# One more column pair by eleven block products in a two-layer streaming encoder step, and a reordered feed of its last projection

## The chip, the core and the metric

The kernel runs on one core of a Trainium2 chip. The metric is device time in microseconds (us) from launch to end, the median of three runs. Beside it stands one profiled execution, with its own time and its span from the first to the last instruction. TensorE is written PE in the rows, its weight load PEld, VectorE DVE, ScalarE ACT, GpSimd POOL, SyncE SP.

## The reference, cut to what matters

Two layers act on 384 token rows: 256 of a prompt (two blocks of 128) and 128 of running streams (one block). Layer 0 is attention of two kinds. Layer 1 is the one that the change touches:

```python
def c_project(h, w_in1, ln_g, ln_b):
    p = jnp.einsum('bsd,dn->bsn', h, w_in1)          # 2048 x 12288
    u = p[..., :C_WIDTH]                             # C_WIDTH = 4096
    v = layernorm(p[..., C_WIDTH:2 * C_WIDTH], ln_g, ln_b)
    z = p[..., 2 * C_WIDTH:]
    return u, v, z
...
mixed = spatial_mix(v, w_sp, b_sp)                   # 128 x 128 causal mixing, 16 groups
hp = hp + jnp.einsum('bsn,nd->bsd', u * mixed * jax.nn.silu(z), w_out1)   # 4096 x 2048
```

So layer 1 is one wide projection, a small mixing of positions, and a second projection back to 2048 columns, added to the layer's input (the residual).

## The kernel before, in words

**Precision.** All inputs are 32-bit floats. Each operand is split in a high and a low half in the matmul's own 32-bit format: ScalarE copies the high half, VectorE subtracts to get the low half, and TensorE adds three products (high by high, high by low, low by high). For 128-row weight blocks of 512 columns that is `wunit` (L79 to L86: `whi` by ScalarE on L84, `wlo` by VectorE on L86) and `products` (L100 to L102). Three token blocks by three products make 9 matmuls for one weight block.

**Column pairs by eleven products.** In layer 1 the weight is taken two column blocks of 512 at a time (columns a0 and a1). For the two prompt blocks, seven products do the work of eight, in the manner of Strassen and Winograd; the stream block needs four ordinary ones, so a pair takes eleven block products where two ordinary column blocks take twelve. This is `seven` (from L959). A product is one token block by half of the 16 weight blocks, 8 of them, by three matmuls: 24 matmuls. Each pair has three parts, each of four units u:

- *singles*: products 1, p, 2 and q; per unit two loads of 128 x 1024, two splits, 24 matmuls;
- *chain*: products 5, s (first half), 6 and 4; per unit four loads, three adds of 128 x 1024 on VectorE (`add`, L968) and three splits, 24 matmuls;
- *pair*: products 3, s (second half) and 7; per unit two loads, one add, two splits, 18 matmuls.

The splits are made by `split` through `split2`: the high half `shi` on L90 (ScalarE), the low half `slo` on L91 (VectorE). Four buffers hold each; the loads (`sraw`) have eight. The parts end with adds that read the product banks. The first of those after the chain reads product 6, and the adds of the pair part are put behind it (`issue_after(second[0])`).

Three pairs are of v columns (`v_pair`), and NP = 5 pairs each join a z block with a u block (`zu_pair`). What is left of z and u is done in ordinary 128-row units (`eight`): four column blocks, z5, u5, z6 and u6, 64 units, loaded through GpSimd's queue. They are dealt out among the units of the chain and the pair parts by the table `mix`, and a scheduler with its own estimates then fixes the order of each engine; no engine reorders at run time. In the built program some 30 ordinary matmuls stand between the chain and the pair part of each pair, where product 6 is awaited, and the rest is spread over the chain and over the start of the next pair.

**The last part.** z7 and u7 are two ordinary column blocks (L1279 to L1285). Meanwhile the gate groups c = 0 to 7 are prepared by generators, `prepare(c)`, eight steps each: loads, three of normalising v, turned mixing weights (L1194), split values, mixing matmuls and gate (L1229 to L1233), stores of the gated rows to DRAM and their read back in blocks (L1236 and L1239, GpSimd's queue), then a turn on VectorE (`gTt`, L1243) and its split into the left operand of the second projection (`slot`, L90 and L91). Tables of hook numbers (`first_plan`, `later_plan`) say behind which weight block a step is written. `out1(k0, nk)` (L1173) runs the second projection over weight rows of two gate groups at a time, four column blocks each, and adds the result to h1 (L1178); h1 comes back from DRAM by `residual_back` on SyncE's queue.

Of the kernel before, what the change touches and what calls it, by code (L numbers as in the profile page):

```python
# [15 lines left out]
P = 128  # L16
DM = 2048
KT = DM // P
NT = 3
# [18 lines left out]
def tile_hybrid_step(  # L38
# [8 lines left out]
    V, S, G, PE = nc.vector, nc.scalar, nc.gpsimd, nc.tensor  # L47
# [121 lines left out]
    with ExitStack() as l0:  # L169
# [200 lines left out]
        for strict in (0, 1):  # L370
# [4 lines left out]
            md = lc.tile([P, TW], F32, name=f"md{strict}")  # L375
# [491 lines left out]
    with ExitStack() as l1:  # L867
# [9 lines left out]
        with ExitStack() as lv:  # L877
# [205 lines left out]
            evict_v(1, dense_nat(w_in1, 0, CW + 512, hh_, hl_, KT, between={kp: lambda q=q: token_sums(q) for q, kp in enumerate((2, 6, 10, 14))}))  # L1083
            NP = 5
            ordinary = [st for c in range(NP, 7) for st in eight(evict_z, c, 2 * CW + c * 512) + eight(evict_u, c, c * 512)]

# [75 lines left out]
        ghi, glo, fgs, aside = [], [], [], {}  # L1162
# [6 lines left out]

        def gk(x, k):  # L1170
            return x[k // 4][:, k % 4, :]

        def out1(k0, nk, between=None):  # L1173
            for c in range(4):
                o = dense_nat(w_out1, k0, c * 512, [gk(ghi, k) for k in range(k0, k0 + nk)], [gk(glo, k) for k in range(k0, k0 + nk)],
                              between={kp: lambda: between.pop(0)() for kp in range(0, nk, 2)} if between else None)
# [32 lines left out]
        def prepare(c):  # L1209
# [24 lines left out]
            yield  # L1234
            for tb in range(NT):
                G.dma_start(md[c][:, tb * P:(tb + 1) * P, :].rearrange("k t d -> t k d"), gate[:, tb, :].rearrange("p (k d) -> p k d", k=4))  # L1236
            blk = lp.tile([P, 4, T], F32, tag="trn", name=nm("blk"))
            for j in range(4):
                G.dma_start(blk[32 * j:32 * j + 32].rearrange("p k (a d) -> p (k a) d", d=32),  # L1239
                            md[c][:, :, 32 * j:32 * j + 32].rearrange("k (a p) d -> p (k a) d", p=32))  # L1240
            yield
# [5 lines left out]
            glo.append(lo)  # L1247

        preps = [prepare(c) for c in range(8)]

# [11 lines left out]
        def times(c, *whens):  # L1262
            return [(c, i) for i in whens]
# [22 lines left out]
        for k0 in (0, 8, 16):  # L1286
            if k0 == 16:
                for j in range(2):
                    fg = slot(F32)[:, :1024]
                    G.dma_start(fg, final_g[j * 1024:(j + 1) * 1024].partition_broadcast(P))  # L1290
                    fgs.append(fg)

                x = slot(F32).rearrange("p (j c) -> p j c", j=3)
                for j, ck in enumerate(order[:3]):
                    aside[ck] = x[:, j, :]
                    G.dma_start(x[:, j, :], wlast(*ck))
            out1(k0, 8, hooked(later_plan(k0 // 4 + 2)))
        wl = {}
# [11 lines left out]

        evicted = out1(24, 4, [lambda: None] * 2 + [last_split] * 3 + [lambda: None] * 3)

# [18 lines left out]
        def last(tb, i):  # L1331
# [4 lines left out]
            for k in range(KL):  # L1336
                hi, lo = wl[c, k]
                gh, gl = gk(ghi, 32 - KL + k)[:, t], gk(glo, 32 - KL + k)[:, t]
# [71 lines left out]
```

## Time and profile before

| | |
|---|---|
| median of three runs | 1756.29 us (1756.17 to 1760.43) |
| profiled execution, its own time | 1759.73 us |
| its span, first to last instruction | 1758.0 us |
| TensorE busy | 1737.2 us, 99% |
| VectorE busy | 1225.6 us, 70% |
| ScalarE, GpSimd busy | 792.6 us, 395.9 us |
| mean granted clock | 0.996 |
| read from memory, written | 357.70 MB, 48.29 MB |

Matmuls are pipelined: a matmul of 512 columns is shown with 390 ns, though the next starts earlier, so the starts give the pace. Idle time stands behind an instruction in brackets with what ended it. The pairs of layer 1 run from about 780 us to 1400 us, z7 and u7 to about 1462 us, the second projection from there to the end.

### The profile page before, as it was taken

The page shows a single profiled execution, that of the slowest core. Times are in us where ns is not written, and L with a number is a line of the kernel's source. Part 1 is how long each engine was busy: PE and PEld are TensorE (multiplying, and loading weights), DVE is VectorE, ACT ScalarE, POOL GpSimd, SP SyncE. Part 2 cuts the span into 40 slices and gives each one's busy share as a digit, 9 for nine tenths or more (in the row PEclk, how much of TensorE's full clock was granted, in tenths as well). Part 3 has the DMA queues.
Part 4 walks back from the last instruction along what each step waited for, and adds up shares of the span by engine and source line. Part 5 has one row for each costly group of instructions (what it writes and reads, how often), then busy time and mean ns, then how long its engine had stood idle before and what let it go on. Part 6 is the DMA issues. An engine that isn't in the chain of part 4 may idle for free. (4 is left out here: it accounts for less than half of the span.)

```text
span 1758.0 us, 24054 instructions
## 1 busy us (share of the span) xinstructions
PE 1737.2 (99%) x8371; PEld 1438.3 (82%) x8371; DVE 1225.6 (70%) x1752; ACT 792.6 (45%) x1239; POOL 395.9 (23%) x581
## 2 busy tenths in 40 slices
PE   9999999999999999999999999999999998999998
PEld 8978888888888888888888888888888887887877
DVE  6437565448348455588788888888788877787766
ACT  5435354337336344454454444545445343333334
POOL 6425545222212201110210010000000233332200
PEclk9999999999999999999999999999999999999999
DMA  8788989868877876678788788877878788878653
GB/s 231 189 222 186 273 228 220 242 178 207 239 200 194 262 197 154 182 272 283 245 262 293 235 281 280 259 262 243 273 258 276 260 271 255 247 223 249 181 144 116
DMA packets 223210, 407.63 MB, mean 232 GB/s; under 512 B 22552, under 2 KB 66128, under 8 KB 223088
## 3 DMA queue, kind: packets, MB, share of 16 engines
q1 hardware_dynamic: 157584, 278.84, 52.7%
q0 software_dynamic: 34672, 111.12, 22.6%
q10 hardware_dynamic: 30832, 16.13, 3.1%
q8 instruction: 65, 1.06, 0.3%
q14 instruction: 57, 0.47, 0.1%
HBM read 357.70 MB, written 48.29 MB: 231 GB/s over the span
## 5 line engine op out<-in xcount | busy, mean ns | idle before, releaser
L101 PE MATMUL d<-wlo,slot 128*128 128x512 f32 x1581 | 616.6, 390 | 2.2 <-DVE wlo L86 2.2
L102 PE MATMUL d<-whi,slot 128*128 128x512 f32 x1581 | 615.2, 390 | 0.0
L100 PE MATMUL d<-whi,slot 128*128 128x512 f32 x1581 | 568.7, 392 | 9.1 <-ACT slot L90 6.1
L86 DVE TENSOR_TENSOR wlo<-raw,whi 128x512 fp32r<-128x512 f32 x514 | 351.7, 696 | 313.3 <-ACT whi L84 309.2
L84 ACT ACTIVATE whi<-raw 128x512 fp32r<-128x512 f32 x514 | 321.6, 629 | 522.1 <-PE d L102 439.0
L100 PEld LDWEIGHTS d<-whi,slot 128*128 128x128 f32 x1581 | 296.8, 188 | 76.1 <-ACT slot L90 6.5
L101 PEld LDWEIGHTS d<-wlo,slot 128*128 128x128 f32 x1581 | 297.4, 188 | 65.2 <-DVE wlo L86 4.3
L102 PEld LDWEIGHTS d<-whi,slot 128*128 128x128 f32 x1581 | 297.0, 188 | 62.0 <-DVE slot L278 0.3
L90 ACT ACTIVATE shi<-sraw 128x1024 fp32r<-128x1024 f32 x224 | 234.7, 1059 | 231.5 <-PE a L957 182.0
L91 DVE TENSOR_TENSOR slo<-sraw,shi 128x1024 fp32r<-128x1024 f32 x224 | 269.2, 1220 | 47.5 <-ACT shi L90 45.2
L956 PE MATMUL a<-slo,slot 128*128 128x512 f32 x640 | 249.0, 389 | 0.0
L955 PE MATMUL a<-shi,slot 128*128 128x512 f32 x640 | 239.7, 389 | 0.0
L957 PE MATMUL a<-shi,slot 128*128 128x512 f32 x544 | 211.6, 389 | 0.0
L968 DVE TENSOR_TENSOR sraw<-sraw,sraw 128x1024 f32<-128x1024 f32 x128 | 154.1, 1220 | 28.3 <-DMA sraw<-in_w_in_dram 28.0
L956 PEld LDWEIGHTS a<-slo,slot 128*128 128x128 f32 x640 | 120.1, 188 | 25.0
L955 PEld LDWEIGHTS a<-shi,slot 128*128 128x128 f32 x640 | 120.1, 188 | 25.0
L74 POOL DMA_DIRECT2D raw<-in_w_in_dram x64 | 35.0, 546 | 397.4 <-DVE wlo L86 375.7
L957 PEld LDWEIGHTS a<-shi,slot 128*128 128x128 f32 x544 | 102.1, 188 | 21.2
L464 POOL DMA_DIRECT2D slot<-d x48 | 44.0, 924 | 140.2 <-DVE wlo L86 54.0
L563 POOL DMA_DIRECT2D slot<-wd x32 | 27.1, 855 | 89.4 <-DMA wd<-pr 41.4
L968 DVE TENSOR_TENSOR slot<-a,slot 128x512 f32<-128x512 f32 x56 | 37.6, 684 | 13.5 <-PE a L957 13.5
L1178 DVE TENSOR_TENSOR slot<-d,slot 128x512 f32<-128x512 f32 x48 | 32.0, 686 | 11.0 <-PE d L102 10.9
(315 smaller groups left out, 1671.3 us busy)
## 6 DMA issues: line engine op xcount, KB each, us to landing
sraw<-in_w_in_dram SPq DMA_DIRECT2D x256, 512.0 KB, 4.9
raw<-in_w_in_dram SPq DMA_DIRECT2D x320, 256.0 KB, 4.0
raw<-in_w_out_dram SPq DMA_DIRECT2D x175, 256.0 KB, 4.2
raw<-in_w_in_dram POOLq DMA_DIRECT2D x64, 256.0 KB, 5.4
slot<-d POOLq DMA_DIRECT2D x48, 192.0 KB, 5.7
d<-slot ACTq DMA_DIRECT2D x24, 256.0 KB, 3.7
vd<-slot POOLq DMA_DIRECT2D x8, 768.0 KB, 6.7
gd<-slot POOLq DMA_DIRECT2D x8, 768.0 KB, 7.3
```

What stands on the lines that cost most here:

```text
L84: highs.append(S.activation(hi, raw, AF.Copy).ins)
L86: splits.append(V.tensor_tensor(out=lo, in0=raw, in1=f32(hi), op=ALU.subtract).ins)
L90: S.activation(hi_out, src, AF.Copy)
L91: V.tensor_tensor(out=lo_out, in0=src, in1=f32(hi_out), op=ALU.subtract)
L100: PE.matmul(o, lhsT=his[k][:, t], rhs=hi[:, 0, :], start=(k == first), stop=False)
L101: PE.matmul(o, lhsT=his[k][:, t], rhs=lo[:, 0, :], start=False, stop=False)
L102: mm = PE.matmul(o, lhsT=los[k][:, t], rhs=hi[:, 0, :], start=False, stop=(k == last))
L464: r = G.dma_start(blk[32 * j:32 * j + 32].rearrange("p h (a d) -> p (h a) d", d=32), d[:, :, 32 * j:32 * j + 32].rearrange("h (a p) d -> p ...
L955: PE.matmul(o, lhsT=xh, rhs=hi[:, j, :], start=(opens and u + j == 0), stop=False)
L956: PE.matmul(o, lhsT=xh, rhs=lo[:, j, :], start=False, stop=False)
L957: PE.matmul(o, lhsT=xl, rhs=hi[:, j, :], start=False, stop=(ends and u == 3 and j == 1))
L968: return V.tensor_tensor(out=out, in0=x, in1=y, op=op)
```

## The change

NP becomes 6: a ninth pair (z5 with u5), and only z6 and u6, 32 units, remain ordinary. `mix` deals one unit to each chain unit (in every third pair three of four) and none to the pair part. In the last part the hook tables are moved: the turn of an odd group goes from the last hook of one `out1` to the second hook of the next (`Late` looks the operand up only when it is used), group 7's turn to the second hook of `out1(24, 4)`; the stores of a group's gated rows are put behind the read back of the group before (`issue_after` on `read`); and the residual comes back later.

```diff
-            NP = 5
+            NP = 6
...
-            for make, c in [(v_pair, c) for c in (2, 4, 6)] + [(zu_pair, c) for c in range(NP)]:
+            for n, (make, c) in enumerate([(v_pair, c) for c in (2, 4, 6)] + [(zu_pair, c) for c in range(NP)]):
...
-                for i, mix in ((1, (2, 2, 2, 1)), (2, (1, 0, 0, 0))):
+                for i, mix in ((1, (1, 1, 1, n % 3 != 1)), (2, (0, 0, 0, 0))):
...
-            for tb in range(NT):
-                G.dma_start(md[c][:, tb * P:(tb + 1) * P, :].rearrange("k t d -> t k d"), gate[:, tb, :].rearrange("p (k d) -> p k d", k=4))
+            with ExitStack() as behind:
+                for i in read:
+                    behind.enter_context(tc.issue_after(i))
+                for tb in range(NT):
+                    G.dma_start(md[c][:, tb * P:(tb + 1) * P, :].rearrange("k t d -> t k d"), gate[:, tb, :].rearrange("p (k d) -> p k d", k=4))
...
-        first_plan = [times(0, 0, 4, 5, 6, 7, 8, 9, 12), times(1, 2, 7, 8, 9, 10, 11, 12, 15), times(2, 13)]
+        first_plan = [times(0, 0, 4, 5, 6, 7, 8, 9, 13), times(1, 2, 7, 8, 9, 10, 11, 12), times(2, 12, 14, 15)]
...
-            return [times(c, 0, 1, 2, 3, 5, 6, 10), times(c + 1, 1, 4, 7, 8, 9, 11, 12, 15)] + ([times(c + 2, 13)] if c < 6 else [])
+            return [times(c - 1, 1), times(c, 2, 3, 5, 6, 13), times(c + 1, 2, 6, 7, 9, 10, 11, 12)] + ([times(c + 2, 10, 14, 15)] if c < 6 else [])
...
-        for i, c in ((5, 0), (7, 1), (9, 2), (11, 3)):
+        for i, c in ((10, 0), (13, 1)):
...
+            for i, c in ((2, 2), (6, 3)) if k0 == 0 else ():
...
-        evicted = out1(24, 4, [lambda: None] * 2 + [last_split] * 3 + [lambda: None] * 3)
+        evicted = out1(24, 4, [lambda: None, lambda: next(preps[7], None)] + [last_split] * 3 + [lambda: None] * 3)
```

The built programs show where the ordinary units went. Counting pairs from 0, the sixteen units of z6 stand before the second unit of pair 1's pair part, fifteen units of u6 between the start of pair 4 and the first units of pair 5's pair part, and the last one from the end of pair 8's chain on. From there in pair 1 to the start of pair 4, and from there in pair 5 to the end of pair 8's chain, TensorE's order has no ordinary matmul: 597 and 774 matmuls of pairs in a row (a pair has 264).

**First place: from the chain to the pair part.** In the program before, TensorE's order in pair 6; `slo_11788` is the low half of the pair part's first weight, `wlo` and `whi` belong to ordinary units:

```order
L956 MATMUL a_11496<-slo_11788,slot_6596 128x512
L957 MATMUL a_11496<-shi_11787,slot_6597 128x512
L955 MATMUL a_11496<-shi_11787,slot_6596 128x512
L956 MATMUL a_11496<-slo_11788,slot_6596 128x512
L957 MATMUL a_11496<-shi_11787,slot_6597 128x512
L101 MATMUL d_11472<-wlo_12084,slot_6999 128x512
L102 MATMUL d_11472<-whi_12082,slot_7000 128x512
L100 MATMUL d_11473<-whi_12082,slot_6999 128x512
L101 MATMUL d_11473<-wlo_12084,slot_6999 128x512
L102 MATMUL d_11473<-whi_12082,slot_7000 128x512
```

The same place in the changed program, again pair 6; `slo_11337` is the low half of the first added weight (product 7), `slo_11333` that of the weight before it:

```order
L956 MATMUL a_11077<-slo_11333,slot_6596 128x512
L957 MATMUL a_11077<-shi_11332,slot_6597 128x512
L955 MATMUL a_11077<-shi_11332,slot_6596 128x512
L956 MATMUL a_11077<-slo_11333,slot_6596 128x512
L957 MATMUL a_11077<-shi_11332,slot_6597 128x512
L955 MATMUL a_11326<-shi_11336,slot_7400 128x512
L955 MATMUL d_11325<-shi_11345,slot_7471 128x512
L955 MATMUL a_11077<-shi_11345,slot_6830 128x512
L956 MATMUL a_11326<-slo_11337,slot_7400 128x512
```

Three matmuls that need high halves alone now stand where the ordinary ones stood; then comes the first that needs the low half. From the last matmul of product 6 to that one there are 21 steps in pairs 3, 6 and 7, and 19 in pair 2.

VectorE's order at this place in the changed program; `a_11078` is product 6:

```order
L968 TENSOR_TENSOR slot_10915<-a_11078,slot_10915 128x512
L968 TENSOR_TENSOR sraw_11329<-sraw_11327,sraw_11329 128x1024
L968 TENSOR_TENSOR sraw_11342<-sraw_11340,sraw_11342 128x1024
L968 TENSOR_TENSOR sraw_11373<-sraw_11371,sraw_11373 128x1024
L968 TENSOR_TENSOR slot_10915<-a_11076,slot_10915 128x512
L968 TENSOR_TENSOR slot_10914<-slot_10915,a_11079 128x512
L968 TENSOR_TENSOR sraw_11404<-sraw_11402,sraw_11404 128x1024
L91 TENSOR_TENSOR slo_11337<-sraw_11329,shi_11336 128x1024
```

Before, the same eight instructions stood here, with the four wide adds next to each other; nothing else moved.

**Second place: GpSimd's queue in the last part.** Before, with `md_7087` the gated rows of group 0, `md_7088` those of group 1, and `blk` the read back:

```order
L1236 DMA md_7087<-gate_12581 128x4x128 x3
L1129 DMA v_13273<-vd_7074 128x1536
L1236 DMA md_7088<-gate_12655 128x4x128 x3
L1239 DMA blk_12941<-md_7087 32x48x32 x4
L1215 DMA gate_13127<-gd_7081 128x1536
L1239 DMA blk_13087<-md_7088 32x48x32 x4
```

And in the changed program:

```order
L1245 DMA md_7087<-gate_12573 128x4x128 x3
L1129 DMA v_13301<-vd_7074 128x1536
L1248 DMA blk_12921<-md_7087 32x48x32 x4
L1245 DMA md_7088<-gate_12647 128x4x128 x3
L1221 DMA gate_13071<-gd_7081 128x1536
L1248 DMA blk_13061<-md_7088 32x48x32 x4
```

The read of group 0 moved ahead of the stores of group 1.

**Third place: VectorE at the start of the second projection.** Before, from the last eviction of u7 (L1284) to the turn of group 1 (the L1243 that ends the piece):

```order
L1284 SCALAR_TENSOR_TENSOR slot_12572<-d_12881,rstd,slot_12572 128x512
L86 TENSOR_TENSOR wlo_13291<-raw_13287,whi_13289 128x512
L86 TENSOR_TENSOR wlo_13297<-raw_13293,whi_13295 128x512
L1140 SCALAR_TENSOR_TENSOR v_13122<-v_13122,mvr,lg_13124 128x512
L1194 STREAM_TRANSPOSE wT_13320<-wr_13129 128x512
L91 TENSOR_TENSOR slot_13081<-gTt_13078,slot_13080 128x1536
L1141 SCALAR_TENSOR_TENSOR v_13122<-v_13122,rsv,lg_13124 128x512
L1195 TENSOR_TENSOR wT_13320<-wT_13320,tri 128x256
L1243 STREAM_TRANSPOSE gTt_13196<-blk_13087 128x1536
```

In the changed program the eviction is L1294 and the turn L1252; the piece between them is longer, and its second half is

```order
L1141 SCALAR_TENSOR_TENSOR v_13066<-v_13066,rsv,lg_13068 128x512
L1201 TENSOR_TENSOR wT_13294<-wT_13294,tri 128x256
L86 TENSOR_TENSOR wlo_13319<-raw_13315,whi_13317 128x512
L86 TENSOR_TENSOR wlo_13325<-raw_13321,whi_13323 128x512
L91 TENSOR_TENSOR vl_13346<-v_13066,vh_13345 128x512 x3
L91 TENSOR_TENSOR wTl_13298<-wT_13294,wTh_13297 128x512
L86 TENSOR_TENSOR wlo_13357<-raw_13353,whi_13355 128x512
L1252 STREAM_TRANSPOSE gTt_13251<-blk_13061 128x1536
```

Group 0's turn moved ahead of the three evictions of u7; ahead of group 1's turn there now stand three more `wlo`, the three `vl`, one `wTl` and two small products of mixing weights (L1194).

More of the change, by code (lines that the diff above doesn't have):

```diff
@@ L1167, in wlast, with __init__, __getitem__ @@
             return w_out1[(32 - KL + k) * P:(33 - KL + k) * P, c * 512:(c + 1) * 512]
-        def gk(x, k):
-            return x[k // 4][:, k % 4, :]
+        class Late:
+            def __init__(self, x, k0):
+                self.x, self.k0 = x, k0
+            def __getitem__(self, k):
+                k += self.k0
+                return self.x[k // 4][:, k % 4, :]
         def out1(k0, nk, between=None):
             for c in range(4):
-                o = dense_nat(w_out1, k0, c * 512, [gk(ghi, k) for k in range(k0, k0 + nk)], [gk(glo, k) for k in range(k0, k0 + nk)],
+                o = dense_nat(w_out1, k0, c * 512, Late(ghi, k0), Late(glo, k0), nk,
                               between={kp: lambda: between.pop(0)() for kp in range(0, nk, 2)} if between else None)
@@ L1234, in prepare @@
             yield
-            for tb in range(NT):
-                G.dma_start(md[c][:, tb * P:(tb + 1) * P, :].rearrange("k t d -> t k d"), gate[:, tb, :].rearrange("p (k d) -> p k d", k=4))
+            with ExitStack() as behind:
[3 more added lines that the diff above has]
+                    G.dma_start(md[c][:, tb * P:(tb + 1) * P, :].rearrange("k t d -> t k d"), gate[:, tb, :].rearrange("p (k d) -> p k d", k=4))
             blk = lp.tile([P, 4, T], F32, tag="trn", name=nm("blk"))
             for j in range(4):
-                G.dma_start(blk[32 * j:32 * j + 32].rearrange("p k (a d) -> p (k a) d", d=32),
-                            md[c][:, :, 32 * j:32 * j + 32].rearrange("k (a p) d -> p (k a) d", p=32))
+                read[:] = [G.dma_start(blk[32 * j:32 * j + 32].rearrange("p k (a d) -> p (k a) d", d=32),
+                                       md[c][:, :, 32 * j:32 * j + 32].rearrange("k (a p) d -> p (k a) d", p=32)).ins]
             yield
@@ L1247, in prepare @@
             glo.append(lo)
+        read = []
         preps = [prepare(c) for c in range(8)]
@@ L1296, in tile_hybrid_step @@
                     G.dma_start(x[:, j, :], wlast(*ck))
-            out1(k0, 8, hooked(later_plan(k0 // 4 + 2)))
+            h = hooked(later_plan(k0 // 4 + 2))
+            for i, c in ((2, 2), (6, 3)) if k0 == 0 else ():
+                h[i] = lambda f=h[i], c=c: [residual_back(c), f()] and None
+            out1(k0, 8, h)
         wl = {}
@@ L1337, in last @@
                 hi, lo = wl[c, k]
-                gh, gl = gk(ghi, 32 - KL + k)[:, t], gk(glo, 32 - KL + k)[:, t]
+                gh, gl = Late(ghi, 32 - KL)[k][:, t], Late(glo, 32 - KL)[k][:, t]
                 PE.matmul(o, lhsT=gh, rhs=hi[:, cs], start=(k == 0), stop=False)
```

## The prediction

> **What bounds the kernel now.** I read the page first, then what TensorE waits for, then the stage of the pairs (TensorE's and VectorE's rows around one part of a pair), then the last part.
>
> The page's head, and from the list of TensorE's waits the two longest (us in total, times, longest):
>
> ```profile
> span 1758.0 us, 24054 instructions
> PE 1737.2 (99%) x8371; PEld 1438.3 (82%) x8371; DVE 1225.6 (70%) x1752; ACT 792.6 (45%) x1239; POOL 395.9 (23%) x581
> ```
>
> ```profile
> PE d L100 <- ACT slot L90: 6.1, 1, 6.1
> PE d L101 <- DVE wlo L86: 2.2, 4, 1.2
> ```
>
> TensorE is the bound and hardly stands still: its longest wait is one of 6.1 us, in the last part. A matmul that goes away is worth its pace, as long as the others keep coming. So two things decide: how many matmuls go, and whether the new order opens holes. The stage of the pairs, one stretch of 100 us (busy PE, PEld, DVE, ACT, POOL, clock, DMA share, GB/s), and from its groups the two wide ones on VectorE:
>
> ```profile
> 1000.00:1100.00 100.00, 100.00 (x443) 82.80 (x442) 86.25 (x94) 47.78 (x54) 11.09 (x20) 1.00 0.83 273
> ```
>
> ```profile
> L91 DVE TENSOR_TENSOR slo<-sraw,shi 128x1024 fp32r<-128x1024 f32 x224 | 269.2, 1220 | 47.5 <-ACT shi L90 45.2
> L968 DVE TENSOR_TENSOR sraw<-sraw,sraw 128x1024 f32<-128x1024 f32 x128 | 154.1, 1220 | 28.3 <-DMA sraw<-in_w_in_dram 28.0
> ```
>
> No hole in TensorE there, but VectorE is at 86%: 224 splits and 128 adds for 8 pairs, 44 wide instructions a pair. It is the engine to watch when a block that costs it little is turned into a pair.
>
> **The work that goes.** z5 and u5 as ordinary blocks are 2 x 144 = 288 matmuls, as a pair 11 x 24 = 264: 24 fewer. The pace, from TensorE's rows at the end of a chain (product 6's last matmul, the last of the weight after it, the first ordinary one, the first with an added weight's low half):
>
> ```profile
> 1298.78 0.39 PE L957 MATMUL a<-shi,slot 128*128 128x512 f32 x1
> ...
> 1302.86 0.39 PE L957 MATMUL a<-shi,slot 128*128 128x512 f32 x1
> 1303.09 0.39 PE L101 MATMUL d<-wlo,slot 128*128 128x512 f32 x1
> ...
> 1311.48 0.39 PE L956 MATMUL a<-slo,slot 128*128 128x512 f32 x1
> ```
>
> From 1298.78 to 1302.86 are 18 steps, 0.2267 us each. So the gain is 24 x 0.2267 = **-5.4 us**, all on the path.
>
> **The entry of the pair part, where the cover goes.** VectorE's rows at the same place:
>
> ```profile
> 1299.21 0.69 DVE L968 TENSOR_TENSOR slot<-a,slot 128x512 f32<-128x512 f32 x1 [0.68 <-PE a L957]
> 1299.82 4.62 DVE L968 TENSOR_TENSOR sraw<-sraw,sraw 128x1024 f32<-128x1024 f32 x4
> 1304.36 0.69 DVE L968 TENSOR_TENSOR slot<-a,slot 128x512 f32<-128x512 f32 x1
> 1304.96 0.68 DVE L968 TENSOR_TENSOR slot<-slot,a 128x512 f32<-128x512 f32 x1
> 1305.55 4.63 DVE L91 TENSOR_TENSOR slo<-sraw,shi 128x1024 fp32r<-128x1024 f32 x4
> ```
>
> The add that reads product 6 waits for TensorE (0.68 us idle); behind it, in VectorE's fixed order, stand four wide adds, two narrow ones and then the first low half. It began at 1305.55 and took, as one of four overlapping ones, 1.2 us: ready at 1306.8, which is 8.0 us after product 6's last matmul started. TensorE asked for it at 1311.48 only, because ordinary matmuls filled 1303.09 to 1311.48. In the changed program these eight instructions of VectorE are the same, so the 8.0 us stay (the scheduler's order, not a unit's length, sets them). But in pairs 2, 3, 6 and 7 no ordinary matmul stands there. TensorE comes to the low half after 21 steps (4.76 us) in three of them and 19 (4.31 us) in one. It stands still for 8.0 - 4.76 = 3.2 us three times and 3.7 us once: **+13.3 us**. Bounds: 12 if the low half runs at the pace of the four, 16 if a load for one of the adds comes late.
>
> **The chain.** The same pair, earlier. Ordinary matmuls in the chain so far (by their high and low weights), TensorE's first use of the low half of unit 2's first weight, and VectorE:
>
> ```profile
> 1273.10:1288.78 15.68, 4.25 (x13) 2.44 (x13) 0.68 (x1) 1.23 (x2) 1.00 0.75 241
> ```
>
> ```profile
> 1273.10:1288.78 15.68, 2.56 (x7) 1.31 (x7) 0.68 (x1) 1.00 0.75 241
> ```
>
> ```profile
> 1288.78 0.40 PE L956 MATMUL a<-slo,slot 128*128 128x512 f32 x1
> ```
>
> ```profile
> 1273.82 1.23 DVE L968 TENSOR_TENSOR sraw<-sraw,sraw 128x1024 f32<-128x1024 f32 x1 [1.03 <-DMA sraw<-in_w_in_dram]
> ...
> 1280.61 1.23 DVE L968 TENSOR_TENSOR sraw<-sraw,sraw 128x1024 f32<-128x1024 f32 x1 [0.96 <-DMA sraw<-in_w_in_dram]
> ...
> 1287.35 4.62 DVE L91 TENSOR_TENSOR slo<-sraw,shi 128x1024 fp32r<-128x1024 f32 x4
> ```
>
> The low half that TensorE takes at 1288.78 was done at 1287.35 + 1.22 = 1288.57: 0.2 us to spare, although 13 + 7 = 20 ordinary matmuls, 4.5 us, had held TensorE up. Without them it would come 4.3 us early; VectorE gets back the one `wlo`, 0.7 us, so TensorE waits 3.6 us. If the two waits for loads (1.03 and 0.96 us) vanish it is 1.6 us; but with no ordinary blocks between, pairs ask for loads faster than at the 0.83 share above, so I rather expect them to stay. I take the middle, 2.5 us a chain, an estimate. Chains without ordinary matmuls are those of pairs 2, 3, 6, 7 and 8: five, **+12.5 us** (8 to 18). A gain I exclude: the wide instructions of a chain stay as they are.
>
> In the other pairs (0, 1, 4, 5, and 8's entry) ordinary units stand as before; I cost them at nothing, that cover being there in the order.
>
> **The last part.** TensorE's 6.1 us wait, with the clock by stretches of 10 us behind it, GpSimd's queue, and VectorE and ScalarE:
>
> ```profile
> 1462.16 0.39 PE L102 MATMUL d<-whi,slot 128*128 128x512 f32 x1
> 1468.62 0.80 PE L100 MATMUL d<-whi,slot 128*128 128x512 f32 x1 [6.07 <-ACT slot L90]
> ```
>
> ```profile
> 1460.00:1470.00 10.00, 3.93 (x15) 2.94 (x14) 8.60 (x13) 2.64 (x3) 0.70 (x2) 0.77 1.04 232
> 1470.00:1480.00 10.00, 10.00 (x41) 8.10 (x40) 8.64 (x11) 5.98 (x9) 3.88 (x7) 0.89 0.92 340
> ```
>
> ```profile
> 1446.59 2.23 POOL L1236 DMA_DIRECT2D md<-gate  x3 [13.73 <-DVE gate L1233]
> 1449.89 3.67 POOL L1239 DMA_DIRECT2D blk<-md  x4 [1.06 <-PE d L102]
> ```
>
> ```profile
> 1463.87 1.37 DVE L1284 SCALAR_TENSOR_TENSOR slot<-d,rstd,slot 128x512 f32<-128x512 f32 x2
> ...
> 1467.23 0.69 DVE L86 TENSOR_TENSOR wlo<-raw,whi 128x512 fp32r<-128x512 f32 x1 [1.40 <-ACT whi L84]
> ...
> 1469.13 1.72 DVE L91 TENSOR_TENSOR slot<-gTt,slot 128x1536 fp32r<-128x1536 f32 x1
> ...
> 1471.76 1.77 DVE L1243 STREAM_TRANSPOSE gTt<-blk 128x1536 f32<-128x1536 f32 x1
> ```
>
> ```profile
> 1467.10 1.47 ACT L90 ACTIVATE slot<-gTt 128x1536 fp32r<-128x1536 f32 x1
> ```
>
> Group 0's operand came late: its read (1449.89) stood behind stores that waited 13.73 us for the next gate. The new order of GpSimd's queue undoes that, and the turn then stands ahead of the evictions. The granted clock of 0.77 and 0.89 is half speed for (0.23 + 0.11) x 10 / 0.5 = 6.8 us, from 1465.4 to 1472.2; TensorE worked 3.6 us of it at half pace, 1.8 us lost. So **-7.9 us** goes here. What is late next: group 0's low half (1.72 us) is still behind u7's last eviction (0.7 us after TensorE's end), while TensorE has six matmuls with the high half, 1.4 us: it waits 1.0 us. Then group 1: its turn ended 1473.53, 8.3 us after the last eviction's end at 1465.2, or 6.9 without the 1.40 us of waiting. Ahead of it now stand three more `wlo`, three `vl`, one `wTl` and two small products, nine narrow instructions, about 4.6 us at 0.5 to 0.6 each: 11.5 us after the eviction, 12.2 after TensorE's end, and its high half (1.47) at 13.7. TensorE needs that half 48 steps after u7's end, 10.9 + 1.0 = 11.9 us: 1.8 us late, and 3.3 if the weights between, which have four buffers, hold VectorE up. I take 3. The last part gives 7.9 - 1.0 - 3.0 = **-3.9 us**, between -7.9 (all hidden) and 0 (as long a hole in a new place). The residual reads move along SyncE's queue away from the first hooks; they hold no one that is late, and I cost them at nothing; if they cover the loads at the start of the second projection, that is inside the 0. Group 7's turn and the later odd groups' stand 8 us ahead of their use: nothing.
>
> **The sum.** -5.4 + 13.3 + 12.5 - 3.9 = +16.5 us. The profiled execution had 1759.73, so 1776.2 by its own time; on the median, 3.4 lower, 1756.29 + 16.5 = 1772.8, say 1773.
>
> **Rivals.**
>
> *The clock drops in the new holes (slower still).* Before, half speed began 2.9 us into the hole that opened at 1462.55 and lasted 6.8 us. If each of the four entries (3.2 to 3.7 us) sets it off, TensorE works at half pace from 3.4 us to 9.7 us after a hole opens: 3.1 us lost each, +12.6 us, 1785. For it: the one long hole did so. Against: the next longest wait in TensorE's list has 1.2 us, so no row shows what 3 us does, and 3.2 is barely more than 2.9. The Trainium skill ("TensorE: Matmul & The Clock Gate", Part 1) has the clock fall to half after an idle window of about 3.4 us that runs freely; by that rule only a hole that happens to fill a window would count, and the trace's 6.07 us hole with its drop agrees.
>
> *VectorE keeps up in the chains.* If the loads come in time and chains lose nothing, +13.3 - 5.4 - 3.9 = +4.0, 1760: within 0.3% (5.3 us, about what can be told from no change here).
>
> *The holes close themselves (faster).* A hole at one entry gives VectorE and the loads 3 us of lead. If they keep it, so that the first entry alone costs 3.2 us and the chains nothing, the sum is -5.4 + 3.2 - 3.9 = -6.1, 1750. It decides below 4 us of holes in all the pairs. Against it: the add on product 6 starts the count anew in each pair, and four buffers for the low halves let VectorE run no further ahead.
>
> **How the numbers follow.** Forecast with its own sizes (about 1764 to 1779) 0.60; clock drops 0.17; chains keep up 0.10; holes close 0.13. The range leaves out the faster case and part of the clock case. Its lower end is the lower bounds with 2 us lost in all chains: -5.4 + 12 + 2 - 7.9 = +0.7, 1757. Its upper end is the upper bounds with nothing gained in the last part, -5.4 + 16 + 18 = +28.6, 1785, and a drop of the clock or two: 1790. Faster by over 0.3% 0.13, within 0.10, slower 0.77.
>
> **What would show it.** TensorE idle before L956 <- DVE `slo` L91, which now is not in its list, with four waits of 3 to 4 us, 60 us apart but for the stretch from pair 3 to pair 6, and smaller ones in chains; VectorE over 90% in stretches without ordinary matmuls; a wait on ACT `slot` L90 of 1 to 3 us in place of 6.07. I am wrong if TensorE shows under 5 us idle in the pairs, or if VectorE's first low half comes sooner than 8 us after product 6.

## The result, and the profile after

The changed kernel takes 1770.49 us (median of 4 runs, 1768.78 to 1774.23), the kernel before 1756.47 in the runs beside it: ratio 1.0078, interval 1.0066 to 1.0091, so 14.0 us slower. The forecast was 1773, slower, in a range of 1757 to 1790. The total is near, but by luck: two of its terms are far off, and they are of opposite sign.

The profiled execution of the changed kernel took 1771.02 us. Its page begins:

```profile
span 1769.3 us, 24022 instructions
PE 1742.9 (99%) x8347; PEld 1439.7 (81%) x8347; DVE 1257.5 (71%) x1773; ACT 804.9 (45%) x1237; POOL 380.9 (22%) x549
```

The 24 matmuls are gone (8371 to 8347), and yet TensorE is busy 5.7 us longer than before (1737.2). Its idle time, span less busy, rose from 20.8 to 26.4 us. So only half of the 11.3 us between the two spans is waiting. The other half has to be slower work.

The waiting first. The three longest of TensorE's list of waits behind the program's start (us in total, times, longest):

```profile
PE a L956 <- DVE slo L91: 12.3, 6, 2.9
PE d L100 <- ACT slot L90: 2.1, 1, 2.1
PE d L102 <- DVE slot L91: 1.0, 1, 1.0
```

The first line did not exist before. Here is its first long entry, in pair 2, in TensorE's rows (start, length, idle time before):

```profile
980.46 0.39 PE L955 MATMUL a<-shi,slot 128*128 128x512 f32 x1
981.26 0.50 PE L955 MATMUL d<-shi,slot 128*128 128x512 f32 x1 [0.41 <-ACT shi L90]
981.60 0.40 PE L955 MATMUL a<-shi,slot 128*128 128x512 f32 x1
984.87 0.50 PE L956 MATMUL a<-slo,slot 128*128 128x512 f32 x1 [2.88 <-DVE slo L91]
...
986.68 0.63 PE L956 MATMUL d<-slo,slot 128*128 128x512 f32 x1
987.11 0.63 PE L957 MATMUL d<-shi,slot 128*128 128x512 f32 x1
```

And VectorE at that place:

```profile
977.26 0.69 DVE L968 TENSOR_TENSOR slot<-a,slot 128x512 f32<-128x512 f32 x1 [1.12 <-PE a L957]
977.87 3.49 DVE L968 TENSOR_TENSOR sraw<-sraw,sraw 128x1024 f32<-128x1024 f32 x3
981.27 0.68 DVE L968 TENSOR_TENSOR slot<-a,slot 128x512 f32<-128x512 f32 x1
...
983.61 3.49 DVE L91 TENSOR_TENSOR slo<-sraw,shi 128x1024 fp32r<-128x1024 f32 x3
```

Both engines ran in the order that the lists under the change give. On VectorE seven instructions stand between the end of the chain and the low half that TensorE needs next (the dots leave out two of them). That low half is ready at 983.61 + 1.22 = 984.83, and TensorE starts on it at 984.87. The same hole of 2.88 us stands in pairs 3, 6 and 7, and in no other pair. Counted from start to start, less one step of 0.2267 us, it is 984.87 - 981.60 - 0.2267 = 3.04 us (the listed idle time begins at a modelled end), and in pair 2 another 981.26 - 980.46 - 0.2267 = 0.57 us stands ahead of it: 4 x 3.05 + 0.57 = 12.8 us for the four entries.

Now the slower work. In the last two of TensorE's rows above the matmuls start 0.43 us apart instead of 0.2267. TensorE by windows of 3.41 us (busy PE, PEld, DVE, ACT, POOL, granted clock, DMA share, GB/s), around the entries of pair 2, pair 6 and pair 7:

```profile
982.57:985.98 3.41, 1.11 (x5) 0.94 (x6) 3.41 (x4) 0.53 (x1) 0.00 (x0) 1.00 0.03 6
985.98:989.39 3.41, 3.41 (x10) 2.67 (x9) 3.38 (x3) 1.06 (x1) 0.00 (x0) 0.50 0.91 270
1262.46:1265.87 3.41, 1.62 (x7) 0.72 (x5) 3.41 (x5) 2.73 (x3) 0.00 (x0) 1.00 0.46 148
1265.87:1272.70 6.83, 5.74 (x14) 4.50 (x15) 5.67 (x5) 1.06 (x1) 0.00 (x0) 0.50 0.61 191
1334.14:1340.96 6.82, 6.07 (x14) 4.78 (x15) 5.33 (x5) 1.06 (x1) 0.00 (x0) 0.50 0.71 217
```

At each of the four holes the clock is halved, for 3.41 us in pairs 2 and 3 and for 6.83 us in pairs 6 and 7. What TensorE worked in these stretches it did at half pace: (3.41 + 3.41 + 5.74 + 6.07) / 2 = 9.3 us lost. In pair 2 the slow stretch begins at 985.98, 1.1 us after work is back. Whoever looks only at waits doesn't see it.

The spells of two windows stand where the hole reaches into the spell: in pairs 6 and 7 TensorE is idle in it for 6.83 - 5.74 = 1.09 us and 0.75 us. In pairs 2 and 3 it works through the first slow window, and no second one follows.

The last part, by the same view over the ten us that hold its longest hole:

```profile
1490.00:1500.00 10.00, 7.90 (x31) 6.21 (x30) 5.11 (x5) 2.39 (x3) 0.53 (x1) 0.83 0.96 317
```

The hole of 6.07 us has become one of 2.10 and one of 1.03, and half a clock for 0.17 x 10 / 0.5 = 3.4 us behind the longer one, 1.7 us lost. Together -6.07 - 1.8 + 1.03 + 2.10 + 1.7 = -3.0 us.

The ledger, from start to start over all of TensorE's rows. In the pairs of the kernel before no step is more than 0.05 us over 0.2267. In those of the changed kernel: the entries 12.8, three other waits 1.7, 18 steps that are 0.05 to 0.35 us too long 2.1, half clock 9.3, less 5.4 for the matmuls: 20.5 us. In the last part: the 3.0 above and 4.6 from small waits on `wlo`, `whi` and the residual adds that are gone or shorter: -7.6 us. Ahead of the pairs, where nothing was changed, this execution took 1.5 us less. That makes 11.4 us; the spans differ by 11.3.

### The profile page after: what moved, and what is told of

It reads as the page before. It is cut to its first block, busy times and chain, and to the rows that moved or that the text cites. A ratio compares the mean times of both kernels' runs of the same rounds, so it can differ in the third digit from the quotient of the medians.

```text
span 1769.3 us, 24022 instructions
## 1 busy us (share of the span) xinstructions
PE 1742.9 (99%) x8347; PEld 1439.7 (81%) x8347; DVE 1257.5 (71%) x1773; ACT 804.9 (45%) x1237; POOL 380.9 (22%) x549
## 5 line engine op out<-in xcount | busy, mean ns | idle before, releaser
L101 PE MATMUL d<-wlo,slot 128*128 128x512 f32 x1485 | 577.8, 390 | 0.0
L102 PE MATMUL d<-whi,slot 128*128 128x512 f32 x1485 | 576.8, 390 | 1.0 <-DVE slot L91 1.0
L86 DVE TENSOR_TENSOR wlo<-raw,whi 128x512 fp32r<-128x512 f32 x482 | 329.5, 695 | 318.8 <-ACT whi L84 314.5
L100 PE MATMUL d<-whi,slot 128*128 128x512 f32 x1485 | 533.2, 392 | 2.8 <-ACT slot L90 2.1
L84 ACT ACTIVATE whi<-raw 128x512 fp32r<-128x512 f32 x482 | 301.7, 630 | 494.4 <-PE d L102 397.2
L90 ACT ACTIVATE shi<-sraw 128x1024 fp32r<-128x1024 f32 x252 | 264.2, 1059 | 275.6 <-PE a L957 216.9
L100 PEld LDWEIGHTS d<-whi,slot 128*128 128x128 f32 x1485 | 279.1, 188 | 64.9 <-ACT slot L90 2.7
L91 DVE TENSOR_TENSOR slo<-sraw,shi 128x1024 fp32r<-128x1024 f32 x252 | 300.6, 1217 | 43.1 <-ACT shi L90 40.1
L102 PEld LDWEIGHTS d<-whi,slot 128*128 128x128 f32 x1485 | 279.0, 188 | 59.9 <-DVE slot L91 1.5
L956 PE MATMUL a<-slo,slot 128*128 128x512 f32 x720 | 283.1, 393 | 12.4 <-DVE slo L91 12.3
L955 PE MATMUL a<-shi,slot 128*128 128x512 f32 x720 | 267.1, 392 | 0.4 <-DVE slot L968 0.4
L957 PE MATMUL a<-shi,slot 128*128 128x512 f32 x612 | 238.5, 390 | 0.0
L968 DVE TENSOR_TENSOR sraw<-sraw,sraw 128x1024 f32<-128x1024 f32 x144 | 173.6, 1219 | 27.0 <-DMA sraw<-in_w_in_dram 26.7
L955 PEld LDWEIGHTS a<-shi,slot 128*128 128x128 f32 x720 | 136.2, 189 | 29.8 <-DVE slot L968 0.9
L957 PEld LDWEIGHTS a<-shi,slot 128*128 128x128 f32 x612 | 115.5, 189 | 24.0
L968 DVE TENSOR_TENSOR slot<-a,slot 128x512 f32<-128x512 f32 x63 | 42.3, 684 | 9.4 <-PE a L957 9.3
L563 POOL DMA_DIRECT2D slot<-wd x32 | 27.1, 855 | 87.5 <-ACT l L733 20.5
(315 smaller groups left out, 1734.2 us busy)
```

The source lines that it names most:

```text
L84: highs.append(S.activation(hi, raw, AF.Copy).ins)
L86: splits.append(V.tensor_tensor(out=lo, in0=raw, in1=f32(hi), op=ALU.subtract).ins)
L90: S.activation(hi_out, src, AF.Copy)
L91: V.tensor_tensor(out=lo_out, in0=src, in1=f32(hi_out), op=ALU.subtract)
L100: PE.matmul(o, lhsT=his[k][:, t], rhs=hi[:, 0, :], start=(k == first), stop=False)
L101: PE.matmul(o, lhsT=his[k][:, t], rhs=lo[:, 0, :], start=False, stop=False)
```

## The experiments

Seven kernels were run. Two theories stood against each other. **A**: VectorE's fixed order at the start of the pair part makes the holes where no ordinary block covers them, and each hole brings a half-clock spell; put the order right and both go. **B**: VectorE has no slack in stretches of pure pair work, so a hole that is closed at one place opens at another. A second question was whether the half-clock records cost what they seem to. All results in one table; busy and idle are TensorE's, from each page, and each ratio is to runs of the kernel before made beside it (their medians are 1756.5 to 1756.9):

| kernel | median us | ratio, interval | span | PE busy | idle |
|---|---|---|---|---|---|
| before | 1756.47 | 1 | 1758.0 | 1737.2 | 20.8 |
| changed | 1770.49 | 1.0078, 1.0066 to 1.0091 | 1769.3 | 1742.9 | 26.4 |
| last part alone | 1752.26 | 0.9975, 0.9966 to 0.9984 | 1752.1 | 1735.9 | 16.2 |
| pairs alone | 1781.06 | 1.0140, 1.0124 to 1.0155 | 1779.3 | 1745.8 | 33.5 |
| adds behind the first low half | 1779.77 | 1.0134, 1.0120 to 1.0148 | 1781.1 | 1747.2 | 33.9 |
| holes filled, 12 matmuls | 1766.09 | 1.0058, 1.0045 to 1.0071 | 1764.0 | 1744.2 | 19.8 |
| holes filled, 5 matmuls | 1768.33 | 1.0062, 1.0039 to 1.0085 | 1766.8 | 1741.0 | 25.8 |
| order of need | 1753.39 | 0.9979, 0.9963 to 0.9996 | 1750.2 | 1734.2 | 16.0 |
| order of need, ten pairs | 1759.06 | 1.0013, 0.9995 to 1.0030 | 1762.3 | 1736.8 | 25.5 |

### The last part alone

The changed kernel with the pairs of before:

```diff
-            NP = 6
+            NP = 5
...
-                for i, mix in ((1, (1, 1, 1, n % 3 != 1)), (2, (0, 0, 0, 0))):
+                for i, mix in ((1, (2, 2, 2, 1)), (2, (1, 0, 0, 0))):
```

> The last part of the changed kernel with the eight column pairs and the mix of the kernel before. The ledger of the two traces (holes and half-clock spells of the last part: 7.9 us before, 1.0 + 2.1 + 1.7 after, and some 3 us of small holes of before that are gone) says that the last part alone gains: -6 to -8 us, about 1749 us (ratio 0.9955 to 0.9965). If the last part's gain came only because the pairs ahead of it had changed the timing of loads and stores, this run stands within 2 us of the kernel before.

Measured 1752.26 us, 0.9975: a gain of 4.4 us by the ratio, less than 6 to 8 but clear of 2. TensorE's waits of the last part in this kernel:

```profile
PE d L100 <- ACT slot L90: 2.1, 1, 2.1
PE d L100 <- ACT whi L84: 1.8, 3, 1.1
```

The first line is the hole of the second gate group, 2.1 us as in the changed kernel. Here no half-clock spell follows it. The small waits on `whi` are still there, 1.8 us as in the kernel before (1.7), where the changed kernel has 0.5. So the last part is a gain by itself, and the loss comes from the pairs.

### The pairs alone

The kernel before with the changed kernel's NP = 6 and `mix` (the first piece above, the other way round).

> The nine pairs with two ordinary blocks between, and the last part of the kernel before. By the ledger: -5.4 for the 24 matmuls, +11.5 for the four entry holes, +10.2 for the half-clock spells behind them, +1.5 for the small holes in the chains, about +18 us: 1774 us (ratio 1.010). If the parts are not separable (the pairs shift the work of the last part), the sum of this run's and the other run's differences is off from +14 by more than 3 us. In the trace: holes of about 2.9 us at the entry of the pair part in pairs 2, 3, 6, 7 as in the changed kernel.

Measured 1781.06 us, 1.0140: a loss of 24.6 us where 18 were expected. With the gain of 4.4 that makes 20.2 for the two parts, and the two together cost 13.7 by the ratio; the parts don't add up, by 6.5 us. The four holes at the entries are there (12.2 us on `slo`). The rest is in the last part, in TensorE's rows

```profile
1478.31 0.39 PE L102 MATMUL d<-whi,slot 128*128 128x512 f32 x1
1484.92 0.79 PE L100 MATMUL d<-whi,slot 128*128 128x512 f32 x1 [6.23 <-ACT slot L90]
...
1555.74 0.39 PE L102 MATMUL d<-whi,slot 128*128 128x512 f32 x1
1558.19 0.50 PE L101 MATMUL d<-wlo,slot 128*128 128x512 f32 x1 [2.06 <-DVE wlo L86]
```

and in the clock (the third column from the end) by stretches of ten us:

```profile
1555.00:1565.00 10.00, 7.37 (x20) 5.06 (x20) 9.19 (x13) 3.67 (x5) 0.00 (x0) 0.70 0.41 127
1565.00:1575.00 10.00, 10.00 (x44) 8.23 (x43) 9.76 (x17) 4.94 (x9) 3.97 (x7) 0.96 0.58 157
```

The long hole of the kernel before is there again, and a wait on `wlo`, 1.2 us at most in the kernel before, is 2.06 us long and brings a spell of its own, (0.30 + 0.04) x 10 / 0.5 = 6.8 us at half clock, up to 3.4 us. All waits on `wlo` L86 together are 4.3 us here and 2.2 in the kernel before, so waits and spell are up to 2.1 + 3.4 = 5.5 of the 6.5. A wait of about 2 us has two prices, with and without the spell.

### Adds behind the first low half

Two narrow additions of the chain and the later wide additions put behind the first low half of the pair part. In this kernel and the two of the order of need, lines stand two higher or three (L970 for L968, L93 and L92 for L91 and L90, L957 to L959 for L955 to L957).

```diff
                 def close_chain():
                     second[:] = [add(v1[:, 0], m["6"], v1[:, 0]).ins]
+
+                def rest_of_chain():
                     add(v1[:, 1], m["5"], v1[:, 0])
                     add(v0[:, 1], v1[:, 0], m["4"], ALU.subtract)
...
-                    with tc.issue_after(second[0]):
+                    with tc.issue_after((low or second)[0]):
                         add(b12, b22, b12)
+                        if u == 1:
+                            rest_of_chain()
                     w, t3 = split2(b22), split2(b12)
+                    if u == 0:
+                        low[:] = lows_made
```

> The changed kernel with two narrow additions of the chain and the later wide additions of the pair part put behind the first low half on VectorE. Theory A (the entry holes come from the order of VectorE's work at the pair part, and each hole drags a half-clock spell behind it): the four holes of 2.9 us go to nothing and the clock of the pairs stays at 1.0, so 11.5 + 10.2 = 21.7 us go, down to about 1749 us (ratio 0.996). Theory B (VectorE has no slack left in stretches of pure pair work, so what is put behind comes up as later waits): the holes come up in the same stretches at other places, the sum of waits on VectorE in pairs 2, 3, 6, 7 falls by less than half, the time by less than 10 us (over 1760).

Measured 1779.77 us, 1.0134: slower than the changed kernel by 9 us, where A had 21 us gained. VectorE in pair 2:

```profile
978.59 0.69 DVE L970 TENSOR_TENSOR slot<-a,slot 128x512 f32<-128x512 f32 x1 [1.10 <-PE a L959]
979.20 1.22 DVE L970 TENSOR_TENSOR sraw<-sraw,sraw 128x1024 f32<-128x1024 f32 x1
981.63 1.23 DVE L93 TENSOR_TENSOR slo<-sraw,shi 128x1024 fp32r<-128x1024 f32 x1 [1.21 <-ACT shi L92]
...
987.37 2.36 DVE L93 TENSOR_TENSOR slo<-sraw,shi 128x1024 fp32r<-128x1024 f32 x2
```

and the two longer of TensorE's three waits there (the first, 0.39 us on ACT `shi`, stands at 982.59):

```profile
985.22 0.50 PE L957 MATMUL a<-shi,slot 128*128 128x512 f32 x1 [0.72 <-ACT shi L92]
988.65 0.50 PE L958 MATMUL d<-slo,slot 128*128 128x512 f32 x1 [2.93 <-DVE slo L93]
```

The first low half was in time: ready at 982.86, taken at 983.17. But everything that had been moved now stood ahead of the second low half, at 987.37, and TensorE waited there: 0.39 + 0.72 + 2.93 = 4.0 us in place of 3.3 (2.88, and a wait of 0.41 ahead of it). VectorE also stood still for 1.21 us, for ScalarE, where a wide addition had fitted before. This is what B says of the place, but it does not prove B: an order that is wrong by one more step looks the same. The half-clock spells grew as well: 3.41 us in pair 2 and 6.83 in each of pairs 3, 6 and 7, 23.9 us in place of 20.5. The last part lost too (two waits on ACT `slot`, 4.7 us, with two spells of 3.41, in place of one wait of 2.1 with one spell); why stays open.

### Holes filled

Needless matmuls at the entry of the pair part in pairs 2, 3, 6 and 7:

```diff
                     def mul():
                         stream(u, w, (m["3"], tsum(3), True, True), (m["s"], row(2, 1), False, True))
+                        if u == 0 and fill:
+                            for _ in range(12):
+                                PE.matmul(m["7"], lhsT=tsum(2)(0)[0], rhs=w[0][:, 0, :], start=True, stop=True)
                         stream(u, t3, (m["7"], tsum(2), True, True))
```

> The changed kernel with 12 needless matmuls of 0.227 us (2.7 us) at the entry of the pair part in pairs 2, 3, 6, 7, into a bank that is opened anew afterwards: they fill the holes and add no wait. Theory A1 (idle time brings the half-clock spells): the holes are filled, no spell follows, and the time falls by 8 to 10 us to about 1761 us (ratio 1.0025). Theory A2 (the spells come from something other than idle time, such as the mix of the work there, or cost nothing): the spells stay in the records or the time stays within 2 us of the changed kernel, 1769 to 1773.

Measured 1766.09 us, 1.0058: 4.4 us less than the changed kernel, where A1 had 8 to 10 and A2 less than 2. The mechanism is A1's. The entries of pairs 2 and 6 by stretches of ten us (pairs 3 and 7 read the same):

```profile
979.00:989.00 10.00, 9.14 (x41) 7.24 (x40) 9.76 (x10) 5.43 (x6) 0.00 (x0) 1.00 0.54 165
1260.00:1270.00 10.00, 9.60 (x43) 7.61 (x42) 9.42 (x10) 4.90 (x6) 0.00 (x0) 1.00 0.58 182
```

The clock is 1.00 there, and holes of 0.86 and 0.40 us are left. TensorE's busy time rose from 1742.9 to 1744.2, though 48 matmuls of 0.2267, 10.9 us, were added: the rest of its work took 9.6 us less, which is the 9.3 us worked out from the half-clock windows. So a half-clock window costs the half that its number says, and idle time brings it on. The expectation missed by a size: it took the filling as free, but 10.9 us of matmuls closed only 6.6 us of idle time.

### Holes filled by less

The same with 5 matmuls, `range(5)`.

> The changed kernel with 5 needless matmuls (1.1 us) at the four entries where the run before had 12, so that holes of about 1.8 to 2.4 us are left. If the half-clock spell follows any hole of about 2 us, the four spells stay and the time stays within 2 us of the changed kernel (1769 to 1773); if it takes more idle time than that, the spells go in some or all of the four places and the time falls by 2.5 us for each short one and 1.7 to 3.4 us for each that it loses: 1762 to 1767 us.

Measured 1768.33 us, 1.0062, between the two. Holes of 2.44 us were left in pairs 2 and 3 and of 1.99 in pairs 6 and 7; spells of 3.41 us followed in pairs 3 and 6 only. The windows of 3.41 us, laid out from the starts of the spells: the one that held most of the hole in pairs 2, 3, 6 and 7.

```profile
983.22:986.64 3.42, 1.85 (x9) 1.20 (x7) 3.42 (x5) 2.52 (x3) 0.00 (x0) 1.00 0.40 136
1048.08:1051.49 3.41, 0.97 (x5) 0.51 (x4) 3.41 (x5) 1.39 (x2) 0.00 (x0) 1.00 0.11 41
1266.54:1269.95 3.41, 1.42 (x7) 1.11 (x7) 3.41 (x4) 0.56 (x1) 0.00 (x0) 1.00 0.14 22
1331.39:1334.80 3.41, 1.67 (x8) 1.05 (x6) 3.41 (x5) 2.00 (x2) 0.00 (x0) 1.00 0.26 99
```

TensorE was idle in them for 1.57, 2.44, 1.99 and 1.74 us; the second and third led to a spell, the first and fourth didn't. Pair 2's hole is as long as pair 3's, but the edge of a window cuts it. In the changed kernel the window 1262.46 to 1265.87 has 3.41 - 1.62 = 1.79 us idle and led to one. So it is not the hole's length that decides but the idle time within one window, and by these rows the border lies between 1.74 and 1.79 of 3.41 us, about half of it.

### The order of need

VectorE's work at the pair part in the order in which TensorE uses it. Wide additions 0 and 1 wait for the chain's first narrow addition alone, as before; each later one waits for the last low half of the unit before, and the two narrow additions stand behind wide addition 2:

```diff
-                    with tc.issue_after(second[0]):
+                    with tc.issue_after(second[0] if u < 2 else lows[u - 1]):
                         add(b12, b22, b12)
+                        if u == 2:
+                            rest_of_chain()
                     w, t3 = split2(b22), split2(b12)
+                    lows[u:] = lows_made
```

> The changed kernel with VectorE's work at the pair part in the order in which TensorE needs it: first narrow addition of the chain, wide additions 0 and 1, the low halves of three tiles, wide addition 2, the other two narrow additions, and so on. Theory A (order alone): the first low half comes some 4.2 us after VectorE has taken up the chain's first addition, where it came 7.6 us after it; the holes of 2.9 us in pairs 2, 3, 6, 7 shrink below 1 us each, no half-clock spell follows, and 16 to 21 us go: 1750 to 1755 us (ratio 0.996 to 0.999). Theory B (VectorE has no slack there): the wait moves on to a later low half of the same part as in the run before, holes of over 2 us remain in at least two pairs, over 1764 us.

Measured 1753.39 us (12 runs, 1749.20 to 1759.04), 0.9979: 17.1 us below the changed kernel, and below the kernel before. VectorE at pair 2 now:

```profile
976.64 0.69 DVE L970 TENSOR_TENSOR slot<-a,slot 128x512 f32<-128x512 f32 x1 [1.28 <-PE a L959]
977.25 2.35 DVE L970 TENSOR_TENSOR sraw<-sraw,sraw 128x1024 f32<-128x1024 f32 x2
979.68 3.50 DVE L93 TENSOR_TENSOR slo<-sraw,shi 128x1024 fp32r<-128x1024 f32 x3
983.09 1.22 DVE L970 TENSOR_TENSOR sraw<-sraw,sraw 128x1024 f32<-128x1024 f32 x1
```

The first low half is ready at 979.68 + 1.22 = 980.90, 4.26 us after VectorE took up the chain's first addition (4.2 expected, 7.6 in the changed kernel). Of TensorE's waits in the pairs there are left:

```profile
PE a L957 <- ACT shi L92: 0.9, 1, 0.9
PE d L957 <- ACT shi L92: 0.8, 2, 0.4
PE a L958 <- DVE slo L93: 0.4, 1, 0.4
```

That is 2.1 us, and no half-clock spell is in the profiled run before its last ten us. A is right and B wrong for nine pairs: VectorE does exactly the same instructions, and their order was worth 17 us. Against the last part alone (1752.26) the ninth pair now neither gains nor loses. From start to start the pairs hold four waits of 2.8 us together and 28 steps that are 0.05 to 0.35 us too long, 3.4 us, where the last part alone has none of either: 6.2 us, which eat the 5.4 of the matmuls.

### Ten pairs in that order

NP = 7, so that z6 and u6 are a pair too.

> The same order of VectorE's work with ten column pairs, so that the last two ordinary blocks become a pair too: 24 matmuls fewer (-5.4 us). Theory A: VectorE keeps TensorE's pace in pure pair work, so the time is 4 to 6 us below the nine pairs in the same order. Theory B: VectorE falls behind when no ordinary block is left between pairs, waits on low halves add up to over 5 us more, and the time is equal or longer than with nine pairs.

Measured 1759.06 us, 1.0013: 5.7 us more than with nine pairs, where A had 4 to 6 less. TensorE's waits in the pairs:

```profile
PE a L957 <- ACT shi L92: 3.7, 5, 1.7
PE d L957 <- ACT shi L92: 2.7, 7, 0.4
PE a L958 <- DVE slo L93: 2.6, 4, 1.1
PE a L957 <- DVE slot L970: 2.5, 3, 1.2
```

11.5 us in place of 2.1, on ScalarE's high halves, VectorE's low halves and the narrow additions alike. Over the stretch 880 to 980 VectorE is nearly full:

```profile
880.00:980.00 100.00, 96.21 (x416) 77.05 (x415) 95.70 (x97) 47.24 (x47) 2.19 (x4) 1.00 0.87 291
```

With nine pairs in the same order it is 90.80 there, and TensorE 99.54: ordinary matmuls of z6 still stand in pair 1 there. B is right by its numbers, over 5 us more of waits and a longer time. But VectorE's load does not say by itself where it falls behind: in the nine pairs' own pure stretch from 978 to 1038 it is busy for 57.71 of 60.00 us, as full as here, and TensorE stands still for 0.94. Counted from start to start, the first three pairs, which now have no ordinary matmul among them, lose 2.6, 5.8 and 3.7 us; pairs 3 to 8 lose 1.0 to 2.5 each, and pure pairs 3 and 7 of the nine 2.4 and 1.6. These figures are from one execution that took 1764.01 us, 5 more than the median, so typical losses are smaller. Which engine's work sets the limit is not shown.

## Why the prediction was right in sum and wrong in two terms

- **The matmuls, -5.4:** right. 24 fewer.
- **The entries, +13.3:** right in place, cause and size, 12.8 from start to start. The four waits are in pairs 2, 3, 6 and 7 and nowhere else; the forecast had 3.2 a hole and 3.7 in pair 2, and they are 3.05 and 3.05 + 0.57. The order of need shows the cause.
- **The chains, +12.5 (8 to 18):** wrong. In the changed kernel the pairs lose 1.7 us in other waits and 2.1 in steps slightly too long, 3.8 us. In the order of need, where no entry hole can hide what the chains lose, it is 2.8 + 3.4 = 6.2 us over all the pairs, below the lower bound of 8 as well. The step that failed is "without them it would come 4.3 us early": it took VectorE's arrival at one low half as fixed and let TensorE alone move up. In pair 6 of the kernel before, TensorE's first matmul of the pair starts at 1248.66 and that low half is ready at 1288.57, 39.9 us later. The same low half in pair 3 of the changed kernel, by TensorE's rows (the pair's first matmul, the first one with this low half) and VectorE's (the second of the two):

```profile
999.54 0.61 PE L955 MATMUL a<-shi,slot 128*128 128x512 f32 x2
...
1032.86 0.39 PE L956 MATMUL a<-slo,slot 128*128 128x512 f32 x1
```

```profile
1029.83 2.35 DVE L91 TENSOR_TENSOR slo<-sraw,shi 128x1024 fp32r<-128x1024 f32 x2
```

  It is ready at 1032.18, 32.6 us after the pair's first matmul and 0.68 us before its use. In pairs 2, 6 and 8 it comes after 32.8 to 33.6 us, 0.4 to 0.6 us before its use; only in pair 7, after 35.2 us, does TensorE wait for it, 0.75 us. So VectorE came 4.8 to 7.3 us sooner than in that pair of before. One reason stands in its waits: up to this low half it waited 5.9 us for loads in pair 6 of the kernel before, and 1.2 to 3.6 us in these five pairs. The prediction had expected those waits to stay; why the loads came sooner is not shown. Pair 6 was also the tightest of the eight pairs: in the others the low half was ready 0.8 to 9.2 us before its use.

  It was a near thing, as a count of VectorE's work shows. Three splits in a row take 3.49 us, so a wide instruction costs VectorE (3.49 - 1.22) / 2 = 1.135 us, and 44 of them 49.9 us; nine narrow additions a pair at 0.6 (977.26 to 977.87) make 5.4, and three to six more narrow instructions on each pair's results 1.8 to 3.6: 57 to 59 us, where a pure pair takes TensorE 264 x 0.2267 = 59.8 us. The row of pair 3, from its first matmul to that of pair 4, has as much:

```profile
999.54:1064.44 64.90, 62.02 (x265) 50.54 (x264) 59.09 (x61) 32.90 (x33) 5.63 (x7) 0.97 0.84 284
```

  VectorE is busy for 59.09 us, 91% of a pair that the entry hole and its spell have made longer, and 99% of TensorE's 59.8.
- **The last part, -3.9:** right for the waits it spoke of, -3.0; the small waits that went beside them, -4.6, were not in the sum. The wait for group 0's low half was forecast at 1.0 and is 1.03; that for group 1 at 3.0 and is 2.10, with 1.7 us of half clock behind it that was not forecast.
- **The clock in the new holes**, a rival with a chance of 0.17 and +12.6 us: true, at +9.3. The argument against it was that a hole of 3.2 us is barely more than the 2.9 us after which the clock had dropped in the kernel before. The 2.9 us were no threshold: they were where the edge of a window happened to lie. The Trainium skill ("TensorE: Matmul & The Clock Gate", Part 1) has the drop after an idle window of about 3.4 us that runs freely. The traces agree on a window of 3.41 us that runs freely, and disagree on the idle time: 1.79 us within one was enough. The hole of 6.07 us, which the prediction took to agree with that rule, did not: the clock fell at 1465.46, when TensorE had been idle for 2.9 us.
- **The other rivals:** "VectorE keeps up in the chains" was true as a mechanism; with the clock's price on top it does not give its 1760. "The holes close themselves" is false: each of the four entries has the same 2.88 us.

So the sum came near by luck: the chains fell short by 12.5 - 3.8 = 8.7 us, and the clock, which was not in the sum, added 9.3. The entries took 0.5 less and the last part gained 3.7 more than forecast: 16.5 - 8.7 + 9.3 - 0.5 - 3.7 = 12.9 us by the two traces, and the medians are 14.0 apart. A sign that the prediction named, VectorE "over 90% in stretches without ordinary matmuls", was true (50.86 of 55.00 us from 991 to 1046, where TensorE has no hole), and did not mean a wait.

## What to carry to other kernels

When a cover goes, don't take a single arrival of the feeding engine as its pace: look at several periods, at what that engine waits for, and at its whole work in a period. Here that work was 57 to 59 us against 59.8, and in the chains it still nearly kept up; the order in which it served the next stage made the long holes. Sort a feeding engine's instructions by when the bound engine needs each of them, not only the first: moving work behind the first low half made things worse, an interleaved order was worth 17 us. Price every hole of TensorE over about 1.8 us with the half-clock spell that it can bring, 1.7 us of work for each window of 3.41 us, and read the clock behind the hole, not in it.

## What the runs showed of the hardware

- The granted clock is decided by windows of 3.41 us: spells are 3.41 or 6.83 us long, and in one execution their starts lie a whole number of windows apart (985.98, 1050.83, 1265.87 and 1334.14 are 19, 63 and 20 windows apart).
- Windows with 1.79 us or more of idle time led to a spell (1.79, 1.99, 2.30 and 2.44 us in the rows above), those with 1.57 and 1.74 us to none. Over all nine traces, laid out in the same way and without the first and last 8 us, 21 windows at full clock with 1.76 us or more led to a spell, and none with 1.75 or less did. The same hole of 2.1 us in the last part brought a spell in the changed kernel and none in the run of the last part alone, where a window's edge parts it into 1.00 and 1.23 us.
- Within a spell less idle time kept the clock down: over the same nine traces, a first half-clock window with 0.57 us idle or more was followed by a second one (8 spells), one with 0.48 or less was not (13 spells).
- A spell begins at the edge of a window, in pair 2 only when the hole is over, so that its loss falls on matmuls that wait for nothing.
